# Where a block's tiles start in SBUF, and which queue stores its hidden rows: both changed in one edit

## The chip, the cores and the metric

The kernel runs on one core of a Trainium2 chip. The metric is device microseconds of one execution, from its first instruction to its last with the launch's own margin. Below, "the profile" is one execution recorded by the hardware profiler; TensorE is called PE, its separate weight load PEld, VectorE DVE, ScalarE ACT, GpSimd POOL and SyncE SP.

## The reference

One transformer block in fp32, batch 1, 512 tokens of width 2048, with 256 context tokens. Cut to what matters:

```
mod = split(silu(c) @ w_ada + b_ada, 6)                    # 2048 x 12288
px  = (norm(x)*(1+sc1)+sh1) @ w_in                         # 512 x 2048 @ 2048 x 7168
pc  = same on ctx, first 4096 columns, only to get start states
ox  = bidirectional gated linear attention of px (8 heads of 128, chunks), gated
loc = pooling mixer (4 windows) and short convolution mixer of px
x   = norm(ALPHA*x + g1*(concat(ox, loc) @ w_out))         # 2048 x 2048
u,g = split((norm(x)*(1+sc2)+sh2) @ w_up, 2)               # 2048 x 11264
h   = u * silu(conv3(g))                                   # 512 x 5632
x   = norm(ALPHA*x + g2*(h @ w_down))                      # 5632 x 2048
```

## The kernel before

**Products.** Every large product is made from fp32 operands that are split into a rounded part (names ending in h: `hxh`, `h2h`, `oh`, `hh`, and for weights `wh_...`, `H_...`) and the remainder (`hxl`, `h2l`, `ol`, `hl`, `wl_...`, `L_...`). `mm3` (L109) then issues three matmuls into the same PSUM bank: rounded times rounded (L111), rounded stationary times moving remainder (L112), stationary remainder times rounded moving (L113). A matmul has a stationary operand of 128x128, which PEld loads before it, and a moving operand of 256 or 512 columns that is streamed past it. Each of the 14,592 matmuls of `mm3` has its own stationary operand, so each comes with a weight load of its own. In a group of the profile `out<-a,b` both operands' names stand without saying which is which; they are told below.

**Stages**, in the order of time:
- *ramp*: first projections of x (`rx`) and of the context (`rc`), with the first modulation (`ada`). 384 + 1152 matmuls of `mm3`.
- *heads and local*: `proj_x` for 25 blocks of 256 columns of w_in, in four pieces each (`wload`, L95, loads and splits a piece). 2112 matmuls have the weights stationary and 512 columns of `hxh`/`hxl` moving; 576 (the v blocks) have `hxh`/`hxl` stationary and 256 columns of weights moving. Between the pieces run the scans and level steps of the attention, and `background` (L652) feeds the rest of the modulation: 256 loads `a` of 128x512 from w_ada, each taken up by DVE (L677).
- *wo*: `out_half`, 768 matmuls, `oh`/`ol` stationary, 512 columns of `wh_wo`/`wl_wo` moving.
- *up_half* (768 matmuls) and *up_pair* (`up_block`, 20 pairs of feature tiles, 6720 matmuls): weights stationary (`H_g`, `L_g`, `H_u`, `L_u`, made by `weights7` and `parts`), 256 columns of activations moving. `up_block` multiplies seven products per pair of blocks; three of the seven take `h2h`/`h2l` as moving operand (2880 matmuls), four take the sums `S1` to `S4` (3840). Each gives a tile of h, which is stored to DRAM (`h_d`; L950 in `up_half`, L1030 in `up_pair`).
- *down* and *finish*: h is loaded again (`load_h`, L1046), split, and used as stationary operand with 512 columns of w_down moving; 2112 matmuls. Of the 44 tiles of h, 30 lie in the `a2` tiles (`hh`/`hl`, 1440 matmuls) and 14 in `hb` tiles (672, the last rows among them).

**Places in SBUF.** Pools stack from the left end (persist, and on it the pools of each stage) and from the right end (`edge`, `acts` with its 34 `a2` tiles of 2 KB, and on it the weight pools `wts` and later `ww`). All big tiles are multiples of 1 KB, so where a pool begins sets where its tiles begin within 128 bytes of a partition's row. Two tiles exist only to shift the rest: `edge_right`, 24 floats, on the right, and `edge_left`, 8 floats, on the left. They put

| tiles | pool | start, bytes past a multiple of 128 |
|---|---|---|
| `h2h`, `h2l`, `hb`, y, K, Q, T, `a` and the other stage tiles on the left | left | 64 |
| `hxh`, `oh`, `S1`..`S4`, `hh`, `hl` and all other `a2` tiles | acts | 0 |
| `wr_`, `wh_`, `wl_`, W, H, L | weight pools | 0 |
| the context's `hch`, `hcl` (they lie behind small tiles) | left | 0 |

So a matmul of `mm3` has one of three pairs of starts, moving/stationary: 0/0 (wo, the projections, `hh`, the S products), 64/0 (`h2h` as moving operand over weights) and 0/64 (weights moving over `hb`).

**Queues.** All DMAs are issued by SP, in the order that the tile scheduler gave; an issue waits for what must be finished before it, and everything behind it on SP waits too. Loads of weights are placed early (`high_priority`), a load of W waits for the L of the block two before it.

Of the kernel before, what the change touches and what calls it, by code (L numbers as in the profile page):

```python
# [9 lines left out]
F32 = mybir.dt.float32  # L10
# [6 lines left out]
P = 128  # L17
# [26 lines left out]
def vw(ap, dims, off=0):  # L44

    return bass.AP(tensor=ap.tensor, offset=ap.offset + off,
                   ap=[list(ap.ap[0])] + [list(d) for d in dims])
# [25 lines left out]
class Kernel:  # L73
    def __init__(self, ctx, tc, I, out):
        self.tc, self.nc, self.I, self.out = tc, tc.nc, I, out
        self.ctx = ctx
        self.persist = ctx.enter_context(tc.tile_pool(name="persist", bufs=1))
        self.edge = ctx.enter_context(tc.tile_pool(name="edge", bufs=1, side="right"))
        self.edge.tile([P, 24], F32, name="edge_right")
        self.acts = ctx.enter_context(tc.tile_pool(name="acts", bufs=1, side="right"))  # L80
        self.dram = ctx.enter_context(tc.tile_pool(name="spill", bufs=1, space=bass.MemoryType.DRAM))
        self.ps = ctx.enter_context(tc.tile_pool(name="ps", bufs=1, space=PSUM))
        self.ahead = 0
# [51 lines left out]
    def setup(self):  # L135
        nc, I, pp = self.nc, self.I, self.persist
        self.ident = pp.tile([P, P], F32, name="ident")
        make_identity(nc, self.ident)
        self.ones = pp.tile([P, 32], F32, name="ones")
        nc.vector.memset(self.ones, 1.0)  # L140
        self.ones_r = pp.tile([P, P], F32R, name="ones_r")
        nc.scalar.copy(out=self.ones_r, in_=vw(self.ones[:, :], [[0, 4], [1, 32]]))
        self.mhalf = pp.tile([P, 4], F32, name="mhalf")
        nc.vector.memset(self.mhalf, -0.5)
        self.zero = pp.tile([P, 1], F32, name="zero")
        nc.vector.memset(self.zero, 0.0)
        self.cols = {}
        self.persist.tile([P, 8], F32, name="edge_left")

    def columns(self, pool, parts, name):  # L150

# [773 lines left out]
    def up_half(self, cp, p, hf):  # L925

        nc, w = self.nc, self.I["w_up"][0]
        banks = self.banks4(f"up_{p}_{hf}")
        n = 256
        for s in (1, 0):  # L930
            for q in (0, 2, 1, 3):
                wh, wl = self.wload(f"up_{p}_{hf}_{s}_{q}",
                                    w[512 * q:512 * q + 512, s * DFF + 256 * p:s * DFF + 256 * p + 256], 4, 256)
                for j in range(4):
                    k = 4 * q + j
                    h, l = self.h2[hf][k // 2]
                    es = slice((k % 2) * 256, (k % 2) * 256 + 256)
                    for i in range(2):
                        self.mm3(banks[2 * s + i][:, 0:n], (wh[:, j, i * P:(i + 1) * P], wl[:, j, i * P:(i + 1) * P]),
                                 (h[:, es], l[:, es]), start=(k == 0), stop=(k == KT - 1))  # L940
        for i in range(2):
            f = 2 * p + i
            u, g = banks[i][:, 0:n], banks[2 + i][:, 0:n]
            c = cp.tile([P, n], F32, name=f"cv_{f}_{hf}", tag="cv", bufs=2)
            s = cp.tile([P, n], F32, name=f"cs_{f}_{hf}", tag="cs", bufs=2)
            self.gate_conv(f, g, c)
            nc.scalar.activation(out=s, in_=c, func=AF.Sigmoid)
            nc.gpsimd.tensor_tensor(out=s, in0=c, in1=s, op=ALU.mult)
            nc.vector.tensor_tensor(out=c, in0=u, in1=s, op=ALU.mult)
            nc.sync.dma_start(out=self.h_d[f][:, hf * 256:hf * 256 + 256], in_=c)  # L950

    def parts(self, ww, name, src, n):

# [60 lines left out]
    def up_pair(self, ww, ep, hx, p):  # L1014
        nc, w = self.nc, self.I["w_up"][0]
        g = self.up_block(ww, ep, f"g{p}", w[:, DFF + 256 * p:DFF + 256 * p + 256])
        cs = []
        for i in range(2):
            f = 2 * p + i
            c = hx.tile([P, 512], F32, name=f"cv_{f}", tag="hq", bufs=8)  # L1020
            s = hx.tile([P, 512], F32, name=f"cs_{f}", tag="hq", bufs=8)
            self.gate_conv(f, g[i], c)
            nc.scalar.activation(out=s, in_=c, func=AF.Sigmoid)
            nc.vector.tensor_tensor(out=c, in0=c, in1=s, op=ALU.mult)
            cs.append(c)
        u = self.up_block(ww, ep, f"u{p}", w[:, 256 * p:256 * p + 256])
        for i in range(2):
            f = 2 * p + i
            nc.vector.tensor_tensor(out=cs[i], in0=u[i], in1=cs[i], op=ALU.mult)
            nc.sync.dma_start(out=self.h_d[f], in_=cs[i])  # L1030

    def down_load(self, dn):

# [203 lines left out]
```

## Time and profile before

| | |
|---|---|
| time, median of 3 runs (lowest, highest) | 2736.46 us (2730.78, 2737.98) |
| the profiled execution: its own time | 2745.75 us |
| its span, first to last instruction | 2743.9 us |
| mean granted TensorE clock | 0.983 |
| busy: PE, PEld, DVE, ACT, POOL | 2589.1, 2271.2, 1891.2, 941.7, 215.8 us |

The profile names an engine's instructions by line, operation, and `out<-in` tiles. The duration of a matmul in it is longer than its distance to the next one, since matmuls are pipelined; rates below are therefore read from starts, not from durations. The profiled execution is 9.3 us above the median of the runs.

### The profile page before, as it was taken

What the parts mean: (1) busy time and instruction counts of PE and PEld (TensorE: products, weight loads), DVE (VectorE), ACT (ScalarE), POOL (GpSimd) and SP (SyncE); (2) the same over time, 40 slices, a digit from 0 to 9 for tenths busy, and PEclk for the clock granted to TensorE, in tenths of its full rate; (3) what the DMA queues carried; (4) which work ended last, traced back from release to release, by engine and by line L of the source; (5) the groups of instructions that cost most, each with busy time, mean ns of one, the idle gap of its engine ahead of it and who ended that gap; (6) DMA issues with size and microseconds to landing.
All of it is one profiled execution on the core that took longest, in us unless ns stands there. A gap on an engine that the chain in (4) does not pass through costs nothing.

```text
span 2743.9 us, 39980 instructions
## 1 busy us (share of the span) xinstructions
PE 2589.1 (94%) x16332; PEld 2271.2 (83%) x16332; DVE 1891.2 (69%) x2390; ACT 941.7 (34%) x1127; POOL 215.8 (8%) x207
## 2 busy tenths in 40 slices
PE   5999999989898999999879999999999999999996
PEld 4677978777787777777879999999999988888885
DVE  5543777585856866677888888988888874434338
ACT  4222532232323223444544434434334433212111
POOL 0111022040403100000100000000000000000004
PEclk9999999999999999999989999999999999999998
DMA  8755344636364466675643333333333365433321
GB/s 266 248 193 176 123 148 147 208 108 195 111 186 140 150 199 171 233 237 164 205 136 115 109 124 123 111 113 123 101 121 114 113 219 180 149 121 102 132 93 62
DMA packets 311124, 416.14 MB, mean 152 GB/s; under 512 B 17860, under 2 KB 200476, under 8 KB 310428
## 3 DMA queue, kind: packets, MB, share of 16 engines
q1 hardware_dynamic: 310940, 413.59, 46.6%
q8 instruction: 128, 2.10, 0.3%
q14 instruction: 56, 0.46, 0.1%
HBM read 393.59 MB, written 19.93 MB: 151 GB/s over the span
## 4 chain that ended last, share of the span: by engine, by line
PE 50%; DMA 20%; DVE 19%; issue 6%; ACT 2%; POOL 2%; SPq 1%; DVEq 0%; POOLq 0%; ACTq 0%
DMA a<-in_w_ada_dram 12%; PE dn L111 5%; PE dn L113 5%; PE dn L112 5%; DMA W_u<-in_w_up_dram 3%; DVE aacc L677 3%; PE ub_g L111 3%; PE ub_g L113 3%; PE ub_g L112 3%; PE ub_u L111 3%; PE ub_u L113 3%; PE ub_u L112 3%; DMA W_g<-in_w_up_dram 2%; DVE L_g L958 2%; PE wo L112 2%
## 5 line engine op out<-in xcount | busy, mean ns | idle before, releaser
L677 DVE SCALAR_TENSOR_TENSOR aacc<-a,csil,aacc 128x512 f32<-128x512 f32 x240 | 184.6, 769 | 166.3 <-DMA a<-in_w_ada_dram 164.0
L958 DVE TENSOR_TENSOR L_dn<-W_dn,H_dn 128x1536 fp32r<-128x1536 f32 (+1 forms) x56 | 96.2, 1718 | 208.8 <-ACT H_dn L957 208.8
L957 ACT CAST H_u<-W_u 128x1792 fp32r<-128x1792 f32 x80 | 134.1, 1691 | 228.0 <-DVE W_u L976 169.8
L111 PE MATMUL dn<-H_dn,hh 128*128 128x512 f32 x480 | 186.7, 390 | 1.9 <-ACT hh L1055 1.9
L958 DVE TENSOR_TENSOR L_u<-W_u,H_u 128x1792 fp32r<-128x1792 f32 x80 | 161.6, 2020 | 37.8 <-ACT H_u L957 37.8
L112 PE MATMUL dn<-L_dn,hh 128*128 128x512 f32 x480 | 187.0, 390 | 0.0
L113 PE MATMUL dn<-H_dn,hl 128*128 128x512 f32 x480 | 186.8, 390 | 0.0
L957 ACT CAST H_g<-W_g 128x1792 fp32r<-128x1792 f32 x80 | 135.2, 1694 | 126.0 <-DVE W_g L976 49.4
L957 ACT CAST H_dn<-W_dn 128x1536 fp32r<-128x1536 f32 (+1 forms) x56 | 81.2, 1451 | 277.6 <-PE dn L113 276.2
L958 DVE TENSOR_TENSOR L_g<-W_g,H_g 128x1792 fp32r<-128x1792 f32 x80 | 161.3, 2018 | 2.3 <-ACT H_g L957 2.2
L111 PE MATMUL ub_g<-h2h,H_g 128*128 128x256 f32 x480 | 135.3, 282 | 15.8 <-ACT H_g L957 15.8
L113 PE MATMUL ub_g<-h2h,L_g 128*128 128x256 f32 x480 | 135.4, 282 | 7.4 <-DVE L_g L958 7.4
L125 POOL TENSOR_TENSOR ln_r<-ln_e,mhalf 128x1 f32<-128x1 f32 x12 | 9.3, 783 | 1649.8 <-DVE ln_e L120 1412.4
L113 PE MATMUL ub_u<-h2h,L_u 128*128 128x256 f32 x480 | 134.6, 280 | 3.0 <-DVE L_u L958 2.9
L111 PE MATMUL ub_u<-h2h,H_u 128*128 128x256 f32 x480 | 134.6, 281 | 0.0
L112 PE MATMUL ub_g<-h2l,H_g 128*128 128x256 f32 x480 | 134.6, 280 | 0.0
L112 PE MATMUL ub_u<-h2l,H_u 128*128 128x256 f32 x480 | 134.0, 279 | 0.0
L106 DVE TENSOR_TENSOR wl_wo<-wr_wo,wh_wo 128x1024 fp32r<-128x1024 f32 x64 | 78.3, 1223 | 49.4 <-ACT wh_wo L105 49.3
L111 PEld LDWEIGHTS dn<-H_dn,hh 128*128 128x128 f32 x480 | 90.1, 188 | 21.6 <-ACT hh L1055 3.0
L113 PEld LDWEIGHTS dn<-H_dn,hl 128*128 128x128 f32 x480 | 90.1, 188 | 19.7 <-DVE hl L1056 1.1
L112 PE MATMUL wo<-wl_wo,oh 128*128 128x512 f32 x256 | 103.0, 402 | 3.7 <-DVE wl_wo L106 3.5
L112 PEld LDWEIGHTS dn<-L_dn,hh 128*128 128x128 f32 x480 | 90.1, 188 | 19.1 <-DVE L_dn L958 0.4
(445 smaller groups left out, 8382.5 us busy)
## 6 DMA issues: line engine op xcount, KB each, us to landing
a<-in_w_ada_dram SPq DMA_DIRECT2D x256, 256.0 KB, 3.3
W_g<-in_w_up_dram SPq DMA_DIRECT2D x80, 512.0 KB, 4.6
W_u<-in_w_up_dram SPq DMA_DIRECT2D x80, 512.0 KB, 4.6
W_dn<-in_w_down_dram SPq DMA_DIRECT2D x24, 1536.0 KB, 6.7
wr_wo<-in_w_out_dram SPq DMA_DIRECT2D x64, 512.0 KB, 4.7
ada<-in_w_ada_dram SPq DMA_DIRECT2D x56, 512.0 KB, 5.1
wr_r<-in_w_in_dram SPq DMA_DIRECT2D x48, 512.0 KB, 3.7
wr_up<-in_w_up_dram SPq DMA_DIRECT2D x32, 512.0 KB, 4.7
```

What stands on the lines that cost most here:

```text
L106: (lo_engine or nc.vector).tensor_tensor(out=lo, in0=raw, in1=hi.bitcast(F32), op=ALU.subtract)
L111: mm(out=out, lhsT=st[0], rhs=mv[0], start=start, stop=False)
L112: mm(out=out, lhsT=st[0], rhs=mv[1], start=False, stop=False)
L113: mm(out=out, lhsT=st[1], rhs=mv[0], start=False, stop=stop)
L125: nc.gpsimd.tensor_tensor(out=r, in0=t, in1=self.mhalf[:, 0:n], op=ALU.pow)
L677: nc.vector.scalar_tensor_tensor(out=acc, in0=raw, scalar=self.csil[:, k:k + 1], in1=acc, op0=ALU.mult, op1=ALU.add)
L957: nc.scalar.copy(out=H[:, 0:n], in_=src)
L958: nc.vector.tensor_tensor(out=Lw[:, 0:n], in0=src, in1=H[:, 0:n].bitcast(F32), op=ALU.subtract)
```

## The change

It does two things. The pads are set anew: `edge_right` shrinks from 24 to 16 floats, `edge_left` goes, and a pool `gap` with a tile of 16 floats is put between `acts` and the weight pools. The left pools move down by 32 bytes, the `a2` tiles up by 32, the weight pools down by 32:

| tiles | before | now |
|---|---|---|
| left pools (`h2h`, `h2l`, `hb`, ...) | 64 | 32 |
| `a2` tiles (`hxh`, `oh`, `S`, `hh`, ...) | 0 | 32 |
| weight pools (`wh_`, `wl_`, W, H, L) | 0 | 96 |
| `hch`, `hcl` | 0 | 96 |

The pairs of starts, moving/stationary, are now 32/96 (weights stationary: 9792 matmuls), 96/32 (weights moving: 3648) and 96/96 (the context's 1152). No tile changes its size, and no tile changes places with another.

And the stores of h, 8 in `up_half` and 40 in `up_pair`, are issued by GpSimd and no longer by SP.

```diff
-        self.edge.tile([P, 24], F32, name="edge_right")
+        self.edge.tile([P, 16], F32, name="edge_right")
         self.acts = ctx.enter_context(tc.tile_pool(name="acts", bufs=1, side="right"))
+        self.gap = ctx.enter_context(tc.tile_pool(name="gap", bufs=1, side="right"))
+        self.gap.tile([P, 16], F32, name="gap_right")
...
-        self.persist.tile([P, 8], F32, name="edge_left")
...
-            nc.sync.dma_start(out=self.h_d[f][:, hf * 256:hf * 256 + 256], in_=c)
+            nc.gpsimd.dma_start(out=self.h_d[f][:, hf * 256:hf * 256 + 256], in_=c)
...
-            nc.sync.dma_start(out=self.h_d[f], in_=cs[i])
+            nc.gpsimd.dma_start(out=self.h_d[f], in_=cs[i])
```

The order of instructions moves as follows. SP, a stretch of the up stage (pairs follow each other; `h_d` are the stores of h, W the loads of weights, the numbers tell the buffers apart), before:

```order
L971 DMA W_g_0_13319<-in_w_up_dram 128x4x256 x2
L971 DMA W_g_1_13417<-in_w_up_dram 128x4x256 x2
L971 DMA W_u_0_13540<-in_w_up_dram 128x4x256 x2
L1030 DMA h_d_93<-cv_13090 128x512
L1030 DMA h_d_94<-cv_13097 128x512
L971 DMA W_u_1_13638<-in_w_up_dram 128x4x256 x2
L971 DMA W_g_0_13751<-in_w_up_dram 128x4x256 x2
```

The same stretch now:

```order
L972 DMA W_g_0_13322<-in_w_up_dram 128x4x256 x2
L972 DMA W_g_1_13420<-in_w_up_dram 128x4x256 x2
L972 DMA W_u_0_13543<-in_w_up_dram 128x4x256 x2
L972 DMA W_u_1_13641<-in_w_up_dram 128x4x256 x2
L972 DMA W_g_0_13754<-in_w_up_dram 128x4x256 x2
```

The two stores between the two loads of W_u are gone; the loads keep their order. SP at the end of `up_half`, where the first W of the up stage is loaded (`wr_up` are the last pieces of `up_half`, `hr` is the first tile of h loaded again), before:

```order
L100 DMA wr_up_1_0_1_11885<-in_w_up_dram 128x4x256
L100 DMA wr_up_1_0_3_11915<-in_w_up_dram 128x4x256
L950 DMA h_d_87<-cv_1_11945 128x256
L950 DMA h_d_88<-cv_1_11954 128x256
L1049 DMA hr_20664<-h_d_85 128x512
L971 DMA W_g_0_12023<-in_w_up_dram 128x4x256 x2
```

Now:

```order
L102 DMA wr_up_1_0_1_11888<-in_w_up_dram 128x4x256
L102 DMA wr_up_1_0_3_11918<-in_w_up_dram 128x4x256
L1050 DMA hr_20667<-h_d_88 128x512
L972 DMA W_g_0_12026<-in_w_up_dram 128x4x256 x2
L972 DMA W_g_1_12124<-in_w_up_dram 128x4x256 x2
```

Only the stores went from in front of the first W_g. POOL at the same place, before (its next work is that of `finish`):

```order
L948 TENSOR_TENSOR cs_1_11946<-cv_1_11945,cs_1_11946 128x256
L948 TENSOR_TENSOR cs_1_11955<-cv_1_11954,cs_1_11955 128x256
L125 TENSOR_TENSOR ln_0_r<-ln_0_e,mhalf 128x1
L1153 TENSOR_TENSOR y_0_20754<-y_0_20754,ln_g_23414 128x512
L1154 TENSOR_TENSOR y_0_20754<-y_0_20754,ln_b_23420 128x512
```

Now:

```order
L949 TENSOR_TENSOR cs_1_11949<-cv_1_11948,cs_1_11949 128x256
L949 TENSOR_TENSOR cs_1_11958<-cv_1_11957,cs_1_11958 128x256
L951 DMA h_d_90<-cv_1_11948 128x256
L951 DMA h_d_91<-cv_1_11957 128x256
L1031 DMA h_d_92<-cv_12229 128x512
L1031 DMA h_d_93<-cv_12236 128x512
L1031 DMA h_d_94<-cv_12661 128x512
```

All 40 stores of the up stage stand on POOL behind each other, with no computation between them. (The number of a line is one or two higher in the changed kernel.)

## The prediction

> **What bounds the kernel now.** I read the page first, then the busy time of each engine stage by stage, then the starts of single matmuls. On the page stand the span, the busy times and the chain that ended last:
>
> ```profile
> span 2743.9 us, 39980 instructions
> PE 2589.1 (94%) x16332; PEld 2271.2 (83%) x16332; DVE 1891.2 (69%) x2390; ACT 941.7 (34%) x1127; POOL 215.8 (8%) x207
> PE 50%; DMA 20%; DVE 19%; issue 6%; ACT 2%; POOL 2%; SPq 1%; DVEq 0%; POOLq 0%; ACTq 0%
> ```
>
> The windows by stage (ramp, heads, local, wo with up_half, up, down, tail) say which engine is full where:
>
> ```profile
> core 0: us, PE busy (x) PEld busy (x) DVE busy (x) ACT busy (x) POOL busy (x), PEclk, DMA share, GB/s
> 30.00:333.00 303.00, 290.17 (x1981) 227.29 (x1982) 151.67 (x211) 99.34 (x140) 32.04 (x25) 0.99 0.60 197
> 333.00:1091.00 758.00, 707.73 (x3834) 590.56 (x3832) 529.17 (x786) 228.52 (x384) 130.16 (x132) 0.98 0.51 159
> 1091.00:1291.00 200.00, 189.77 (x817) 151.53 (x816) 141.42 (x198) 87.59 (x105) 2.64 (x4) 0.97 0.66 215
> 1291.00:1414.00 123.00, 99.71 (x802) 96.28 (x801) 104.61 (x153) 61.48 (x90) 14.27 (x12) 0.93 0.58 183
> 1414.00:2232.00 818.00, 807.15 (x6717) 804.59 (x6718) 707.52 (x715) 337.07 (x283) 0.00 (x0) 1.00 0.36 118
> 2232.00:2719.00 487.00, 485.11 (x2116) 396.26 (x2115) 217.14 (x246) 113.20 (x106) 16.64 (x12) 1.00 0.38 130
> 2719.00:2744.00 25.00, 0.53 (x3) 0.09 (x1) 20.17 (x29) 3.04 (x4) 17.12 (x13) 0.56 0.29 105
> ```
>
> PE is busy 807 of 818 us in the up stage and 485 of 487 in the down stage: there, 1305 us together, the rate of its matmuls is the time. In the heads stage it is idle for 50 of 758 us, because another chain ends last now and then:
>
> ```profile
> DVE aacc L677 <- DMA a<-in_w_ada_dram: 164.0, 113, 4.1
> ```
>
> (us in total, times, longest.) A saving on a matmul there reaches the end only where PE is the last; I count half, with nothing and all of it as the ends.
>
> So the question is what one matmul costs, and whether the places of its operands enter. Durations don't tell, since matmuls overlap; starts do. PE's timeline at four places, first and last row of an unbroken run of equal matmuls (start in us, modelled duration, line, operands): S products, then h2h products of the same output, then hh and hb in the down stage.
>
> ```profile
> 1698.90 0.28 PE L111 MATMUL ub_g<-S3h,H_g 128*128 128x256 f32 x1
> ...
> 1700.94 0.28 PE L113 MATMUL ub_g<-S2h,L_g 128*128 128x256 f32 x1
> 1701.06 0.28 PE L111 MATMUL ub_g<-h2h,H_g 128*128 128x256 f32 x1
> ...
> 1703.06 0.28 PE L113 MATMUL ub_g<-h2h,L_g 128*128 128x256 f32 x1
> ...
> 2299.90 0.39 PE L111 MATMUL dn<-H_dn,hh 128*128 128x512 f32 x1
> ...
> 2309.88 0.39 PE L113 MATMUL dn<-H_dn,hl 128*128 128x512 f32 x1
> ...
> 2404.78 0.40 PE L111 MATMUL dn<-H_dn,hb 128*128 128x512 f32 x1
> ...
> 2414.82 0.39 PE L112 MATMUL dn<-L_dn,hb 128*128 128x512 f32 x1
> ```
>
> - S (0/0, 256 columns): 17 steps in 2.04 us, 120.0 ns each.
> - h2h (64/0, 256 columns): 17 steps in 2.00 us, 117.6 ns.
> - hh (0/0, 512 columns): 44 steps in 9.98 us, 226.8 ns.
> - hb (0/64, 512 columns): 43 steps in 10.04 us, 233.5 ns.
>
> S and h2h have the same weights tiles, the same form and the same output, and no wait lies between them: they differ in where the moving operand lies, and by 2.4 ns. hh and hb differ in where the stationary one lies, and by 6.7 ns. The two 0/0 rates give the streaming alone, (226.8 - 120.0)/256 = 0.417 ns a column, and what is left over it in each class: 120.0 - 106.8 = 13.2 ns for 0/0, 10.8 for 64/0, 19.9 for 0/64. These leftovers, not the streaming, are what the new places can change.
>
> **The change, part by part.** *The pads.* Not one of the new pairs (32/96, 96/32, 96/96) occurs in the trace, so their price is bounded by the three that do: between the 64/0 row and the 0/64 row, and below it, if all of a leftover can go. I take the 64/0 row, 2.4 ns below 0/0, for every pair that is now 64 bytes apart, in both roles. Of the two comparisons it is the clean one: one thing differs. hb differs from h2h in three at once (role, columns, which operand is off its line), so its surcharge can't be pinned on the distance, which the two share. That is a choice, and the rivals price the others. Term by term, with the counts of the stages:
>
> - S, 3840 matmuls, 0/0 becomes 32/96: 3840 x 2.4 ns = 9.2 us, all on the path (up stage).
> - h2h, 3648 matmuls, were 64 apart and still are: 0.
> - hh, 1440 matmuls, 0/0 becomes 96/32: 1440 x 2.4 = 3.5 us, on the path (down stage).
> - hb, 672, 0/64 becomes 96/32: from 233.5 to 226.8 - 2.4 = 224.4, so 672 x 9.1 = 6.1 us, on the path.
> - Projections in heads and local, 2112 + 576 = 2688: 6.5 us, half counted: 3.2.
> - wo, 768: 1.8; rx, 384: 0.9, both nearly full of PE work. rc, 1152, two equal starts as before (0/0, now 96/96): 0.
>
> Sum 9.2 + 3.5 + 6.1 + 3.2 + 1.8 + 0.9 = 24.7 us. What is late next in the up stage if PE gets 9.2 us shorter? DVE is busy 707.5 of 818 us, 110 us of cover, and PE's own waits there are small:
>
> ```profile
> PE ub_g L111 <- ACT H_g L957: 15.8, 1, 15.8
> PE ub_g L113 <- DVE L_g L958: 7.4, 4, 2.5
> ```
>
> The first is the one entry into the stage, before any of this; the second could grow by a few us, and that goes into the range. Small DVE and ACT operations and the DMAs also get new starts: the trace has DVE operations from 64 and from 0 side by side and they take alike, as the next fence shows for one (0.69 us for 128x512), so 0.
>
> *The stores of h.* Each leaves SP and goes to POOL. Place in a pair where SP had them (SP's timeline, start and duration of a group), and DVE's in the same us:
>
> ```profile
> 1828.69 1.54 SPq L1030 DMA_DIRECT2D h_d<-cv  x2
> 1831.83 0.94 SPq L971 DMA_DIRECT2D W_u<-in_w_up_dram  x2
> ```
>
> ```profile
> 1829.18 0.69 DVE L1029 TENSOR_TENSOR cv<-Z_u,cv 128x512 f32<-128x512 f32 x1
> 1829.78 2.02 DVE L958 TENSOR_TENSOR L_g<-W_g,H_g 128x1792 fp32r<-128x1792 f32 x1
> ```
>
> The load of W_u behind the stores starts at 1831.83, and the L that frees its buffer ends at 1829.78 + 2.02 = 1831.80: it waited for L, not for the stores. Their removal frees nothing: gain 0, at most what PE idles in the whole stage, 818.0 - 807.2 = 10.8 us. On POOL they stand behind no work (0.00 us busy in the stage) and hold up nothing. Who waits for a store? Its landing took 2.0 us (the third row, KB and median us), and the loads of h follow each other in the order of the tiles, to the last:
>
> ```profile
> L1030 SPq DMA_DIRECT2D h_d<-cv x40: 319/338/393, 1463.0 to 2241.1; - x40
> L1049 SPq DMA_DIRECT2D hr<-h_d x44: 319/390/1972, 1400.6 to 2520.0; - x44
> h_d<-cv SPq DMA_DIRECT2D x40, 256.0 KB, 2.0
> ```
>
> The last store is issued at 2241.1 and the last load at 2520.0, 279 us of cover. The trace shows no DMA on POOL. If issuing one held DVE for as long as a store takes to land, it would be 40 x 2.0 = 80 us of the 110 that DVE has free, thus still 0 but for a delay of some L by up to 2 us; I take 0, from -3 to +3.
>
> [...]
>
> Together: 24.7 us off the profiled execution's 2745.75 gives 2721.1; that execution is 9.3 above the median of the runs, so **2712** on the scale of the median. This case's own range: down to 2696 if the projections count in full (3.2 more), the stores bring 3 and S gains twice as much (9.2 more); up to 2725 if the projections count for nothing (3.2 less), wo too (1.8), the stores cost 3 and waits on L eat 5.
>
> **The rivals.** A measurement of this kernel tells 0.3%, 8.2 us, from no change.
>
> - *Leftovers shrink by more* (faster). With both operands off the start of a 128-byte line, half of each leftover may go: 13.2/2 = 6.6 ns for S, hh, wo and the ramp without rc (3840 + 1440 + 768 + 384 = 6432: 42.5 us), 10.8/2 for h2h (3648: 19.7), 13.2/2 and half of it for the projections (8.9), 19.9/2 for hb (6.7): about 78 us, 2658. In the up stage that is 41 of 818 us (25.3 for S, 15.6 for 2880 of h2h), which DVE's 707.5 still allows. For it: 64/0 shows that a leftover can shrink. Against: by 18% only.
> - *Each role keeps its own price* (no change). h2h and hb were both 64 apart, and one gained as moving operand while the other lost as stationary operand. If that stays so, S gains 9.2 and the projections half of 2112 x 2.4, 2.5, but hh loses 1440 x 6.7 = 9.6, wo 768 x 6.7 = 5.1 and the v projections half of 576 x 6.7, 1.9: +4.9 us, 2741. For it: it takes both rows as they are. Against: it needs roles that differ for a reason the trace doesn't name.
> - *Places don't matter to PE* (no change). Then the 2.4 and 6.7 ns come from something else, and the time stays at 2736. Against it: S and h2h stand within one run of 36 steps with nothing else different. [...]
> - *A stationary operand off its line is the cost* (slower). hb is the only class whose stationary operand doesn't begin at a multiple of 128, and the only slow one; now none does. At hb's surcharge of 6.7 ns: S and h2h, 7488 x 6.7 = 50.2 us, hh and wo 2208 x 6.7 = 14.8, half the projections 9.0, the ramp 1536 x 6.7 = 10.3, in all 84 us: 2820. It decides against the change from 8.2 us on, at 84/6.7 = 12.6 thousand matmuls that is 0.65 ns each, a tenth of hb's surcharge. For it: PEld is busy 804.6 of 818 us in the up stage, so a weight load that takes longer has no room. Against: hb's own group doesn't show whether 64 stands for 32 and 96.
>
> **How the numbers follow.** Forecast 0.37; larger gain 0.12; roles keep their price 0.12; places don't matter 0.08; stationary off its line 0.31. Faster 0.37 + 0.12 = 0.49, same 0.12 + 0.08 = 0.20, slower 0.31. The range takes in the larger gain's 2658 and the slow case to its 2820, with 3 us for the stores: 2655 to 2823. Left out are larger gains than half a leftover and a surcharge above hb's. As gain and loss both carry weight, the likeliest case's 2696 to 2725 stands beside it.
>
> **What would show it.** Starts in the same four runs: right if S comes to 117.6, hh and hb to about 224.4 and h2h stays; the stores on POOL with the W_u load still starting at the end of L, and no `hr` load later than now. Roles keep their price if hh goes to 233.5; the slow rival if S goes above 123 and h2h above 120; places don't matter if all four stay, hb with hh apart. The forecast is wrong, whatever the time, if S and h2h no longer run alike, or if PE's waits on L in the up stage grow beyond 20 us.

## The result, and the profile after

| | before | changed |
|---|---|---|
| median, us (4 runs each, same chip) | 2736.42 | 2763.51 |
| lowest, highest | 2730.78, 2737.98 | 2758.97, 2771.85 |
| ratio, 95% interval | | 1.0106 (1.0077 to 1.0135) |
| profiled execution, span | 2743.9 | 2763.5 |

The change made the kernel 1.1% slower, 27 us by the medians and 19.6 us between the two profiled executions (the one of before lies 9.3 us above its median, the one after 1.8 above). The page of the changed kernel says little: PE is busy 7 us longer, POOL 32.

```profile
PE 2596.0 (94%) x16332; PEld 2256.4 (82%) x16332; DVE 1889.0 (68%) x2390; ACT 938.9 (34%) x1127; POOL 247.4 (9%) x255
```

The starts of the stages say more. Up runs from the first `ub_g` matmul to the first `dn` matmul, down from there to the last matmul; in the windows of the changed kernel:

```profile
core 0: us, PE busy (x) PEld busy (x) DVE busy (x) ACT busy (x) POOL busy (x), PEclk, DMA share, GB/s
1409.00:2239.50 830.50, 805.86 (x6721) 797.82 (x6722) 707.68 (x715) 334.38 (x282) 20.72 (x38) 0.99 0.35 116
2239.50:2738.60 499.10, 495.20 (x2114) 397.47 (x2112) 217.13 (x246) 113.10 (x106) 17.87 (x14) 1.00 0.37 127
```

Before, up ran from 1414.4 to 2232.4 and down to 2719.1 (both ends are starts of matmuls). So up went from 818.0 to 830.5 (+12.5), down from about 486.7 to 499.1 (+12.4), and everything ahead of up got 5.4 us shorter (1414.4 to 1409.0). That is 19.5 of the 19.6 us. In up, PE is idle for 24.6 us (830.5 - 805.9), where it was for 10.9.

Most of *down* is explained by the starts of single matmuls. PE's timeline of the changed kernel, first and last of a run of S, of hh and of hb:

```profile
1497.05 0.28 PE L113 MATMUL ub_g<-S4h,H_g 128*128 128x256 f32 x1
...
1498.93 0.28 PE L114 MATMUL ub_g<-S1l,H_g 128*128 128x256 f32 x1
...
2299.68 0.39 PE L115 MATMUL dn<-H_dn,hl 128*128 128x512 f32 x1
...
2309.95 0.39 PE L114 MATMUL dn<-L_dn,hh 128*128 128x512 f32 x1
...
2419.62 0.39 PE L113 MATMUL dn<-H_dn,hb 128*128 128x512 f32 x1
...
2429.89 0.39 PE L115 MATMUL dn<-H_dn,hb 128*128 128x512 f32 x1
```

S: 16 steps in 1.88 us, 117.5 ns, as forecast (120.0 before). hh: 44 steps in 10.27 us, 233.4 ns, where 226.8 stood before and 224.4 was forecast. hb: 44 steps in 10.27 us, 233.4, unchanged, where 224.4 was forecast. hh alone is 1440 x 6.6 = 9.5 us. Most of the other 3 us is lost near the start of the stage, where PE waits longer for `hh` (the changed kernel, then the one before; us in total, times, longest):

```profile
PE dn L113 <- ACT hh L1056: 3.9, 2, 2.5
```

```profile
PE dn L111 <- ACT hh L1055: 1.9, 2, 1.4
```

Behind the wait of 2.5 us, seven steps from matmul to matmul take 427 ns each, not 233.

*Up* is another matter, since S did get faster there (3840 x 2.5 = 9.6 us) and the stage still got longer. The waits of the changed kernel, over the whole run (us in total, times, longest):

```profile
DVE W_u L975 <- DMA W_u<-in_w_up_dram: 46.7, 38, 3.0
...
PE ub_u L115 <- DVE L_u L959: 17.9, 18, 2.7
...
PE ub_g L115 <- DVE L_g L959: 6.6, 5, 2.1
```

and of the kernel before:

```profile
DVE W_u L974 <- DMA W_u<-in_w_up_dram: 35.0, 38, 2.7
...
PE ub_u L113 <- DVE L_u L958: 2.9, 3, 1.2
```

PE waits for the remainder `L_u` in most pairs now, and DVE waits longer for the load of `W_u` that it is made from, 46.7 - 35.0 = 11.7 us in 38 waits. From the first `ub_g` matmul of a pair to that of the next it is 39.57 us now where PE has no wait, and 40.05 before. Before, 12 of the first 19 pairs are like that; now it is four, the pair that begins at 1530.3 takes 41.2 us and the next ones 42.1, 42.6 and 44.2.

### The profile page after: what moved, and what is told of

Read it like the earlier page. It is cut to its first block, busy times and chain, and to the rows that moved or that the text cites. A ratio compares the mean times of both kernels' runs of the same rounds, so it can differ in the third digit from the quotient of the medians.

```text
span 2763.5 us, 40050 instructions
## 1 busy us (share of the span) xinstructions
PE 2596.0 (94%) x16332; PEld 2256.4 (82%) x16332; DVE 1889.0 (68%) x2390; ACT 938.9 (34%) x1127; POOL 247.4 (9%) x255
## 4 chain that ended last, share of the span: by engine, by line
issue 34%; PE 34%; DMA 15%; DVE 11%; POOL 2%; ACT 2%; SPq 0%; DVEq 0%; POOLq 0%; ACTq 0%
DMA a<-in_w_ada_dram 13%; PE dn L115 5%; PE dn L114 5%; PE dn L113 5%; DVE aacc L678 3%; PE wo L114 2%; PE wo L115 2%; PE wo L113 2%; PE rc L113 1%; PE rc L115 1%; PE ada L282 1%; PE rc L114 1%; PE up L115 1%; DVE A L649 1%; PE up L114 1%
## 5 line engine op out<-in xcount | busy, mean ns | idle before, releaser
L115 PE MATMUL ub_u<-h2h,L_u 128*128 128x256 f32 x480 | 137.8, 287 | 18.1 <-DVE L_u L959 17.9
L115 PEld LDWEIGHTS ub_u<-h2h,L_u 128*128 128x128 f32 x480 | 90.9, 189 | 23.3 <-DVE L_u L959 23.1
```

Source lines behind the costliest of these rows:

```text
L115: mm(out=out, lhsT=st[1], rhs=mv[0], start=False, stop=stop)
```

## The experiments

Two things had to be told apart: what the places do to PE, and what the stores on POOL do to the loads. Each kernel was run beside the kernel before on the same chip (e1 to e4 on one, e5 to e8 on one, e9 to e12 on one); the ratio is to that. "Up" is the up stage of its profiled execution, from the first `ub_g` matmul to the first `dn` matmul.

| run | what | ratio (95%) | median, beside before | up, us |
|---|---|---|---|---|
| e1 | pads alone | 1.0010 (0.9996 to 1.0024) | 2730.98, 2727.87 | 808.2 |
| e2 | stores alone | 1.0025 (1.0009 to 1.0041) | 2734.06, 2727.87 | 813.2 |
| e3 | all at 32, stores SP | 0.9987 (0.9975 to 0.9998) | 2724.88, 2727.87 | 816.8 |
| e4 | 0 and 64, stores SP | 1.0021 (1.0001 to 1.0041) | 2729.23, 2727.87 | 810.6 |
| e5 | the changed kernel again | 1.0109 (1.0088 to 1.0131) | 2767.8, 2738.32 | 837.1 |
| e6 | first store POOL, second SP | 1.0028 (1.0008 to 1.0047) | 2742.62, 2738.32 | 807.2 |
| e7 | first store SP, second POOL | 1.0025 (1.0008 to 1.0043) | 2744.97, 2738.32 | 809.4 |
| e8 | distance by columns, stores SP | 0.9987 (0.9969 to 1.0006) | 2735.12, 2738.32 | 812.7 |
| e9 | all at 32, both stores POOL | 1.0020 (1.0004 to 1.0036) | 2732.04, 2728.27 | 822.3 |
| e10 | e8, gate product on POOL | 1.0054 (1.0037 to 1.0072) | 2744.54, 2728.27 | 831.9 |
| e11 | the kernel before, one execution | | 2726.56, 2728.27 | 809.5 |
| e12 | second store: 64 columns on POOL | 1.0011 (0.9995 to 1.0027) | 2730.48, 2728.27 | 804.1 |

**e1, the pads alone.** The changed kernel with

```diff
-            nc.gpsimd.dma_start(out=self.h_d[f], in_=cs[i])
+            nc.sync.dma_start(out=self.h_d[f], in_=cs[i])
```

and the same for the stores of `up_half`.

> The new pads alone; the stores of h stay on SP. Theory 1 (the stores on POOL delay the loads of W_u, and that costs the up stage its gain): the up stage gets shorter than before, 818 us less about 10, and only the down stage and wo lose, some 12 and 2 us; the time comes to 2730 to 2740. Theory 2 (PE runs faster with the new places, and the chain of loads, casts and remainders can't follow, whoever stores): the up stage keeps its 830 us and the time stays at 2755 to 2765. In both, hh is at 233.4 ns and S at 117.5.

The up stage falls to 808.2 us (its window follows) and the time is 2730.98: theory 1. Down takes 494.2 us, 7.5 more than before where 12 had been expected; the rest of the 12.4 comes with the stores (below). By itself the new layout costs 0.1%, which can't be told from nothing: S gains about what hh and wo lose.

```profile
1399.70:2207.90 808.20, 798.93 (x6721) 797.25 (x6722) 708.52 (x715) 337.15 (x282) 0.00 (x0) 0.99 0.36 120
```

**e2, the stores alone.** The kernel before, with `nc.gpsimd` in place of `nc.sync` for the stores of h.

> The stores of h on POOL alone; all tiles start where they did before. Theory 1: the second load of W_u of a pair lands later, PE waits for L_u as in the changed kernel, and the up stage takes 10 to 20 us longer than 818; the time 2746 to 2758. Theory 2: PE is as slow as before, so nothing is late: 2734 to 2738. S stays at 120.0 ns, hh at 226.8.

It came out between the theories: 0.25%, and an up stage of 813.2, which lies between the 809.5 and 818.0 of the two executions of the kernel before. Down takes 490.1 us, 3.4 more than before. The two halves alone make 0.35% together, the whole 1.06%.

**e5, the changed kernel again**, to see whether that gap is one of the chip.

> The changed kernel once more, beside runs of the kernel before on the same chip. Theory I (the two halves interact: with the new places a pair of the up stage takes 39.6 us and leaves the loads less time, and with the stores on POOL a W_u lands late): the ratio stays near 1.010, and most pairs of the up stage show PE waiting for L_u. Theory A (the halves add, 0.1% and 0.25%, and the first chip was a bad one for this kernel): the ratio is 1.002 to 1.005, and stalls come in a few pairs only.

1.0109: theory I. The halves interact, on another chip too.

**e3 and e4, other places.** e3 is e1 without the pad `gap_right`; e4 is e1 with `edge_right` 24 and an `edge_left` of 24 floats.

> Left tiles, a2 tiles and weights all at 32, stores on SP: no pair of big tiles is 64 apart. Theory D (only the distance of the two starts counts, and a distance of 64 helps at 256 columns and hurts at 512): S and h2h both at 120.0 ns, hh, hb and wo at 226.8 to 227; hb gains 672 x 6.6 = 4.4 us, h2h loses 3648 x 2.4 = 8.8; about 2741. Theory R (what counts is that the stationary operand begins off a 128-byte line): hh, hb and wo at 233.4, and the time at 2750 or more.

> Left and a2 tiles at 0, weights at 64, stores on SP: the same distance as in the changed kernel, other places. Theory D: every rate as with 32 and 96 (S and h2h 117.5 ns, hh, hb and wo 233.4, the v projections about 115), and the time that of the new pads alone. Theory R: as the stationary operands of hh, hb and wo now begin on a line, these run at 226.8, and S and h2h, whose weights don't, above 120.

Theory D holds for S and hh in both. In e3, where nothing is 64 apart though no big tile begins on a line, S is back at 120.0 ns (20 steps in 2.40 us, from 1499.51 on) and hb falls to 226.5 (37 steps in 8.38 us):

```profile
2399.83 0.39 PE L112 MATMUL dn<-L_dn,hb 128*128 128x512 f32 x1
...
2408.21 0.39 PE L113 MATMUL dn<-H_dn,hb 128*128 128x512 f32 x1
```

In e4, where the stationary operands of hh do begin on a line, hh is as slow as with 32 and 96 (43 steps in 10.04 us, 233.5 ns), and S is at 117.8 (23 steps in 2.71 us):

```profile
1498.50 0.28 PE L113 MATMUL ub_g<-S4h,H_g 128*128 128x256 f32 x1
...
1501.21 0.28 PE L115 MATMUL ub_g<-S2h,L_g 128*128 128x256 f32 x1
...
2299.77 0.40 PE L114 MATMUL dn<-L_dn,hh 128*128 128x512 f32 x1
...
2309.81 0.39 PE L115 MATMUL dn<-H_dn,hl 128*128 128x512 f32 x1
```

So, for S and hh, it doesn't matter where the tiles begin; how far the two operands' starts are apart does. But the distance modulo 128 bytes is not all of it. In e4 hb is 64 apart as it was before, and theory D said 233.4; it runs at 229.0 ns (107 steps in 24.50 us):

```profile
2389.13 0.40 PE L113 MATMUL dn<-H_dn,hb 128*128 128x512 f32 x1
...
2413.63 0.40 PE L115 MATMUL dn<-H_dn,hb 128*128 128x512 f32 x1
```

The second and third pair of e4 take 38.99 us, below the 39.57 of the changed kernel, because h2h runs at about 114 ns there. The changed kernel has the same two sizes: read by their starts, its 512-column projections run at 228.9 ns and hh and wo at 233.3, its v projections mostly at 113.3 and S and h2h mostly at 117.8, and all of them are 64 apart. With 256 columns every class that is 64 apart was faster than 120.0, and with 512 slower than 226.8; which of two sizes it gets is not explained here. e3's time is 0.13% below the kernel before, where 4 us more had been worked out: down gained 3 us of the 4.4 worked out for hb (483.6), the pairs of up take 40.32 us as they should, and the stages ahead of up are 4 us shorter than in e11; why is open.

**e6 and e7, one store of a pair each.** The changed kernel with

```diff
-            nc.gpsimd.dma_start(out=self.h_d[f], in_=cs[i])
+            (nc.gpsimd if i == 0 else nc.sync).dma_start(out=self.h_d[f], in_=cs[i])
```

and, in e7, the two engines the other way round.

> The changed kernel, but of the two stores of a pair only the first is issued by POOL; the second goes back to SP. In the changed kernel the first store is issued at once and the second 2.05 us after, when DVE's L_g ends, together with the load of W_u. Theory L (this late second store is what costs): the time is that of the new pads alone, within 0.2%. Theory I or A without it (any store on POOL costs its share): half of the loss against the new pads alone stays.

> The reverse: the first store by SP, the second by POOL. Theory L: the second is again issued only when L_g ends, W_u lands late, and the time is that of the changed kernel within 0.2%. The other theory: half of the loss, as with the first store alone on POOL.

e6 is as theory L says, 807.2 us in up and 1.0028. e7 speaks against it as it was put: the second store alone on POOL should have been as dear as both, and costs as little as the first, 1.0025. Its rows show why. POOL, then DVE, in a pair of e7:

```profile
1534.93 0.54 POOL L1031 DMA_DIRECT2D h_d<-cv  x1 [39.59 <-DVE cv L1030]
```

```profile
1533.85 0.69 DVE L1030 TENSOR_TENSOR cv<-Z_u,cv 128x512 f32<-128x512 f32 x1
1534.45 2.02 DVE L959 TENSOR_TENSOR L_g<-W_g,H_g 128x1792 fp32r<-128x1792 f32 x1
1536.38 0.69 DVE L977 TENSOR_TENSOR W_u<-W_u 128x512 f32<-128x512 f32 x1
```

The store is issued 0.39 us after its product, in the middle of L_g: a single store on POOL is not held up by DVE. Only the second of two on POOL comes late. The stores of the third pair in the changed kernel (POOL, then DVE):

```profile
1541.23 0.54 POOL L1031 DMA_DIRECT2D h_d<-cv  x1 [38.95 <-DVE cv L1030]
1543.83 0.54 POOL L1031 DMA_DIRECT2D h_d<-cv  x1 [2.06 <-issue]
```

```profile
1541.35 0.69 DVE L1030 TENSOR_TENSOR cv<-Z_u,cv 128x512 f32<-128x512 f32 x1
1541.95 2.02 DVE L959 TENSOR_TENSOR L_g<-W_g,H_g 128x1792 fp32r<-128x1792 f32 x1
...
1550.00 1.23 DVE L975 TENSOR_TENSOR W_u<-W_u 128x1024 f32<-128x1024 f32 x1 [1.52 <-DMA W_u<-in_w_up_dram]
```

and in e1, with both stores on SP:

```profile
1529.84 2.02 DVE L959 TENSOR_TENSOR L_g<-W_g,H_g 128x1792 fp32r<-128x1792 f32 x1
...
1536.97 1.23 DVE L975 TENSOR_TENSOR W_u<-W_u 128x1024 f32<-128x1024 f32 x1 [0.60 <-DMA W_u<-in_w_up_dram]
```

The second store's product is done at 1541.35 + 0.69 = 1542.04, and POOL issues it at 1543.83, 2.60 us behind the first. What it waits for is the landing of the first store, 2.3 us after that one's issue. In the five traces with two stores of a pair on POOL (the changed kernel, e2, e5, e9, e12; 24 pairs each, with those of `up_half`) the second starts 0.30 to 0.32 us after the first has landed, in every pair, though the two are 2.33 to 6.41 us apart. The profile names most of these waits "issue" or an operation of DVE; in the last pair it names the store, and DVE is in the middle of an L (POOL, then DVE):

```profile
2248.00 0.54 POOL L1031 DMA_DIRECT2D h_d<-cv  x1 [33.37 <-DVE cv L1030]
2250.59 0.54 POOL L1031 DMA_DIRECT2D h_d<-cv  x1 [2.04 <-DMA h_d<-cv]
```

```profile
2249.61 1.76 DVE L959 TENSOR_TENSOR L_dn<-W_dn,H_dn 128x1536 fp32r<-128x1536 f32 x1 [0.20 <-ACT H_dn L958]
```

On SP, before, the second store goes out 1.2 us behind the first, which lands only 2.0 us after its issue.

From the end of L_g, which frees the buffer of W_u, to the first use of the new W_u it takes 1550.00 - 1543.97 = 6.03 us in the changed kernel and 1536.97 - 1531.86 = 5.11 us in e1: 0.92 us more. Over 19 pairs the median of this round trip is 5.8 to 6.0 us in the four runs with both whole stores on POOL (the changed kernel, e2, e5, e9) and 5.2 to 5.3 us in the ten others. What the DMA engines move in these us (windows; the last two columns are their busy share and GB/s), in the changed kernel:

```profile
1541.23:1542.73 1.50, 1.50 (x15) 1.50 (x14) 1.50 (x3) 0.00 (x0) 0.54 (x1) 1.00 0.28 106
1542.73:1545.00 2.27, 2.27 (x22) 2.27 (x21) 1.84 (x2) 0.27 (x1) 0.54 (x1) 1.00 0.12 45
1545.00:1547.00 2.00, 2.00 (x20) 2.00 (x19) 0.55 (x1) 2.00 (x2) 0.00 (x0) 1.00 0.83 280
1547.00:1549.40 2.40, 2.40 (x23) 2.40 (x22) 1.48 (x1) 1.39 (x2) 0.00 (x0) 1.00 0.89 313
```

and in e1:

```profile
1528.75:1530.25 1.50, 1.50 (x15) 1.50 (x14) 1.50 (x3) 0.00 (x0) 0.00 (x0) 1.00 0.44 167
1530.25:1532.90 2.65, 2.65 (x24) 2.65 (x24) 2.21 (x2) 0.28 (x1) 0.00 (x0) 1.00 0.31 110
1532.90:1534.40 1.50, 1.50 (x15) 1.50 (x14) 0.06 (x1) 1.41 (x1) 0.00 (x0) 1.00 0.84 253
1534.40:1536.40 2.00, 2.00 (x19) 2.00 (x18) 1.97 (x1) 0.53 (x1) 0.00 (x0) 1.00 0.97 334
```

In e1 the first two windows move 167 x 1.50 + 110 x 2.65 = 542 KB, which is both stores (2 x 262), and the last two 1.50 x 253 + 2.00 x 334 = 1048 KB, the two loads of W_u (1049). In the changed kernel the first two move 261 KB, one store, and the last two 2.00 x 280 + 2.40 x 313 = 1311 KB: the loads and the second store. The store's bytes go in the middle of the load, and the load takes 4.4 us where it took 3.5.

**e12, the bytes or the DMA.** The changed kernel, with the second store cut in two:

```diff
+            if i == 0:
+                nc.gpsimd.dma_start(out=self.h_d[f], in_=cs[i])
+            else:
+                nc.sync.dma_start(out=self.h_d[f][:, 0:448], in_=cs[i][:, 0:448])
+                nc.gpsimd.dma_start(out=self.h_d[f][:, 448:512], in_=cs[i][:, 448:512])
```

> The changed kernel, but of the second store of a pair POOL issues only 64 of the 512 columns, and SP the other 448. POOL still has two DMAs in a pair, the second again 2.6 us behind the first. Theory B (the bytes of the late second store lie in the way of W_u's load): nearly all bytes now go early, W_u lands as with one store on POOL, and the time is 1.001 to 1.004 of the kernel before. Theory Q (a second DMA on POOL costs by itself, by what it holds on GpSimd or VectorE): the loss stays near 1.010.

1.0011, and an up stage of 804.1, the shortest of all: theory B. POOL still issues two DMAs in a pair, the second 2.6 us or more behind the first, but the late one is small. (Down takes 499.0 us as in the changed kernel.)

**e9, the same stores and a slower PE.** e3 with the stores on POOL.

> All big tiles at 32 (no pair 64 apart; alone, with the stores on SP, this layout took 0.9987 of the kernel before), and now both stores of h on POOL. W_u lands 0.7 to 0.9 us later, as in the changed kernel. Theory S (what the stores cost depends on how long PE takes for a pair, and here it takes 40.3 us where the changed kernel takes 39.6): the loss is like that of the stores alone, 0.1% to 0.4% against this layout without them, so 1.000 to 1.003 of the kernel before. Theory P (it is the new start addresses, or the missing pad, that make the stores dear): about 1% against this layout without them, 1.007 to 1.010.

1.0020, that is 0.33% above e3: theory S. Its pairs take 40.32 us without a wait, and all of the second to the eleventh do. W_u is late here too, with a round trip of 5.8 to 6.0 us; a PE that needs 0.75 us more for a pair doesn't notice until the others' stalls come as well.

**e8 and e10, towards a better version.** e8 is e1 with the weights of the 512-column products moved by 64 bytes inside their tiles (to 32), by these lines in `parts`, and the like in `wload`:

```diff
+        o = 16 if name[:2] in ("dn", "rs") else 0
+        H, Lw = H[:, o:], Lw[:, o:]
```

> The new pads with the stores on SP, but the weights of every product with 512 columns (projections, wo, down, finish) start 64 bytes further in their tiles, at 32, where the activations start; the products with 256 columns keep the distance of 64. Theory D (distance 64 helps at 256 columns and hurts at 512): S, h2h, v projections at 117.5, 117.5 and 115 ns, hh, hb and wo at 226.8; against the kernel before S gains 9, hb 4.5, the v projections half of 3 us: 0.5% faster, about 2714 where the kernel before has 2728, unless the loads of the up stage don't follow.

Down takes 483.8 us, with hh and hb at 226.7 ns, and S runs at 117.7; but the time is 0.9987, with an interval that reaches past 1. The projections and wo didn't come down to 227 ns but change between about 227 and 233 (the edit also makes their tiles 128 bytes longer, which puts every second one at another place modulo 256), the v projections ran at 117.8 and not 115, and up took 812.7 us, with waits in 12 of 19 pairs: what PE saves there, it waits. e10 adds

```diff
-            nc.vector.tensor_tensor(out=c, in0=c, in1=s, op=ALU.mult)
+            nc.gpsimd.tensor_tensor(out=c, in0=c, in1=s, op=ALU.mult)
```

> The layout with the distance by columns (256 columns 64 apart, 512 columns equal), stores on SP, and the two gate products of a pair (128x512 each, 1.4 us a pair) on POOL, no more on DVE. If DVE's load is what lets the up stage stall once PE is faster, the stalls get fewer and the time falls below 0.9987 of the kernel before, to 0.994 or 0.996. If what limits is the round trip of a load (the landing, the cast, the remainder) or POOL's product is late, it stays or gets worse.

It got worse: up takes 831.9 us. DVE has 40 operations fewer in up and is busy longer, 719.4 us against 707.5 in e8, and the product takes 1.3 to 2.9 us on POOL (median 2.3) where DVE took 0.68. That DVE's load as such lets the stage stall is not borne out, though the run is no clean test, since it slows DVE too. It does show that a run of waits can come without stores on POOL.

**e11, the kernel before once more.**

> The kernel before again, for its up stage on this chip: some of the 20 pairs at 40.05 us, and a few episodes of 1 to 4 us in which PE waits for a remainder.

Two episodes, in the first pair and at 1846 to 1933 us, and 40.05 us in all others; up 809.5 where the first execution had 818.0. Every kernel here has waits between about 1840 and 2000 us; what differs is whether they begin at about 1530 already (the changed kernel, its repetition, and e10). e4, with its stores on SP, has two long pairs from 1566 on, 42.1 and 43.8 us, and is back at 39.57 in the next.

## Why the prediction was wrong, point by point

The forecast was 2712 with a range of 2655 to 2823. The measured 2763.51 lies inside the range, on the other side of no change. Slower had been given 0.31, but for a cause that e3 rules out, so that the range holds the time is luck.

- *What bounds the kernel.* Right: PE's rate sets up and down. A pair without waits went from 40.05 to 39.57 us, 0.48 x 20 = 9.6 us for the stage.
- *S, 9.2 us saved; h2h, 0.* Right: 117.5 ns for S by the run shown, 117.8 over most of S and of h2h.
- *hh 3.5, wo 1.8, hb 6.1 us saved.* The first failing step: "I take the 64/0 row, 2.4 ns below 0/0, for every pair that is now 64 bytes apart, in both roles." At 512 columns 64 apart costs hh and wo over 6 ns instead. hh lost 9.5 us, hb gained nothing, wo lost (from 227 to 233.3 ns by its starts). hb's surcharge had been called impossible to pin on the distance; e3, with equal starts, took it away (226.5 ns). Of the three things in which hb and h2h differ, it is the number of columns that turns the sign, not the role: the v projections, with 256 columns and the weights moving like hb's, gained from 64 apart, and the 512-column projections, with the weights stationary like S's, lost (from 227 to 228.9 ns by their starts, where a gain of 2.4 had been counted). The v projections by modelled durations, the row of before, then of after:

```profile
L111 PE MATMUL px_v<-wh_x_v,hxh x192: 278/283/582, 446.1 to 786.6; 128*128 128x256 f32 x192
```

```profile
L113 PE MATMUL px_v<-wh_x_v,hxh x192: 276/276/384, 445.4 to 783.2; 128*128 128x256 f32 x192
```

- *The rival "each role keeps its own price"* had hh and wo right (233.4 was its 233.5) and the sum of the layout, +4.9 us; e1 measured 0.1%, 3 us. Its reason, the role, was not the one: by it the 512-column projections should have gained. *The rival "a stationary operand off its line"* named the sign of the result and nothing else of it: e3, all off their line, shows no such cost (S at 120.0 ns, hb at 226.5). *The rival "places don't matter to PE"* was wrong: the places do matter, 120.0 against 117.5 ns and 226.8 against 233.4 by the two starts alone (the run that the prediction calls 36 steps is 36 matmuls, 35 steps). Which part of the loading or the streaming it is that depends on them, no run shows.
- *The stores, 0, from -3 to +3.* The second failing step, and the largest error of a single term. "Their removal frees nothing" was right; "Who waits for a store?" had two answers that were missed. The first is the next store: on POOL the second of a pair goes out only when the first has landed (0.30 to 0.32 us after it), and then its bytes take DMA time from a load that DVE waits for. On SP the bytes of both stores had gone before those of W_u began to flow (1532.9 in e1); on POOL the second goes 2.6 us behind the first and into the load. The 110 us that DVE has free in the stage were no cover, since what got longer is one round trip (load, products, cast, remainder), not DVE's work (707.7 us in up, 707.5 before). Alone the stores cost 0.25%; with the faster PE, 1.0%, as e1 and e5 bound it (1.0010 and 1.0109). The range had 5 us for waits on L; they ate 22 (808.2 to 830.5). PE's waits on L in up are 17.9 + 6.6 = 24.5 us, beyond the 20 that the prediction itself had named as a sign of being wrong.
- The second answer is SP, at the end of up. Its first load of `g` waits until the last store has landed, and all loads behind it on SP wait too (SP's waits from 2242 to 2258 us in the changed kernel; us in total, times, longest):

```profile
SPq L1041 <- DMA h_d<-cv: 10.1, 2, 7.6
```

  The last store of the changed kernel lands at 2252.88 and `g` goes out at 2252.96; it is so in the kernel before too, but `g` goes out earlier in the stage there (12.0 us after the first `dn` matmul, now 13.5), and three loads of h that follow in the same us go out at 25.9, 28.3 and 33.6 us after it, where they went out at 23.3, 25.3 and 31.2. With the first store of a pair on POOL (the changed kernel, e2, e5, e6, e9, e12) PE's longest wait for `hh` is 2.5 to 3.1 us, in the other eight at most 1.5: that is most of what is left of down's 12.4 us. The 279 us of cover were read from the last load of h, and the first ones are the ones that count.
- What DVE does at the time is not what makes these stores late. A single store, in e7, was issued during L_g, 0.39 us after its product, and in the changed kernel a second one comes 0.30 to 0.32 us after the first has landed whether DVE works at that moment (20 of 24 pairs) or not (4).

What makes the first load late that starts a run of waits is shown by time only, not by an experiment. In the changed kernel it is a W_g that DVE waits for until 1561.5, for 2.4 us, at the same pair in both executions. While that load is under way, one packet of the queue that the profile calls "instruction" (16 KB, 2.46 us) begins at 1555.7; from 1559 on the load's last bytes flow at 20 to 26 GB/s, where they flowed at 350 to 400 (40 equal slices of 1554.8 to 1561 us, then the queue's packets, MB and share):

```profile
GB/s 0 0 0 0 0 145 165 159 192 211 251 192 304 357 350 357 377 357 344 363 383 357 390 403 370 311 212 60 26 20 26 20 26 26 20 26 26 20 26 0
q8 instruction: 1, 0.02, 2.5%
```

In the fourteen traces, from 1450 us to the end of up, DVE waits over 1.9 us for a load of W_u or W_g 83 times. In 82 of them such a packet had begun within 4.5 us of the load's issue, while only 370 of all 1023 loads have one. No run moved these packets. With the round trip 0.9 us longer and the pair 0.5 us shorter the stage does not get over such a load; e4, with a round trip of 5.2 us, does.

## What to carry to other kernels

A transfer whose data nobody needs soon had a price here where its bytes met a load that somebody waits for (4.4 us for the load of W_u where it took 3.5): ask of a store that is moved not only who needs it but what its new queue waits for between two transfers, and what else the DMA engines carry at its new time. In this stage, where PE's pair got shorter (40.05 to 39.57 us) and the round trip of a load longer (5.11 to 6.03 us in the third pair), two small changes cost more than their sum, 1.0106 together and 1.0010 and 1.0025 alone; measure such changes one by one and together. And a rate that was read at one shape (256 columns) is a guess at another, above all when the trace already holds a row of the other shape with the opposite sign: 64 apart, S went from 120.0 to 117.5 ns and hh from 226.8 to 233.4.

## What the runs showed of the hardware

- The distance of the two operands' starts modulo 128 bytes changes the pace of back-to-back matmuls of this kernel's form (a weight load each): 0 apart 120.0 ns at 256 columns and 226.8 at 512 (0/0 as 32/32, in e3), 64 apart 117.8 or 113.3 and 233.3 or 228.9. The distance doesn't decide it alone: 64 apart gave two paces at each shape, and in e8 products that are 0 apart ran at up to 233. What else counts stays open.
- GpSimd issued the second of two DMAs 0.30 to 0.32 us after the first had landed, in all 120 pairs of five traces; SP issues its second store 1.2 us behind the first, which lands after 2.0. A store of the up stage landed 2.3 us after its issue by GpSimd where it was the first of a pair and 3.7 where it was the second (medians), and 2.0 us after that by SP. Over all 40 of the changed kernel:

```profile
h_d<-cv POOLq DMA_DIRECT2D x40, 256.0 KB, 3.1
```

- A load of 1 MB in which a 16 KB packet of the queue "instruction" began could leave DVE waiting for over 1.9 us: 82 of 83 such waits, as counted above.
- After a wait of 1.98 us in the changed kernel, up to 1727.8, PE ran at half its clock for 3 us, one matmul each 213 ns; a window in it:

```profile
1728.00:1731.00 3.00, 3.00 (x16) 3.00 (x16) 2.83 (x5) 0.67 (x1) 0.00 (x0) 0.51 0.69 218
```

  The granted clock, 0.51, made this stall dearer than its wait: 15 matmuls at 213 instead of 117.5 are 1.4 us more.
